# One image's store of a Winograd convolution, cut into transfers of 96, 24 and 8 channels

## The chip, the cores and the metric

The kernel runs on one core of one Trainium2 chip. The metric is the device time in microseconds, the median of several runs. One run was taken with the hardware profiler; its trace and profile page are what this document reads.

A core has five engines with instruction queues of their own: TensorE (PE, its weight loads PEld), VectorE (DVE), ScalarE (ACT), GpSimd (POOL) and SyncE (SP). Data moves by sixteen DMA engines, which all queues share. A transfer is issued from SP, ACT or POOL and cut into rows that are dealt out to the DMA engines; each DMA engine has a ring for each queue. In the profile, q1 is SP's queue, q10 ScalarE's, q0 GpSimd's; q8 and q14 bring instructions.

## The reference

A 3x3 convolution with padding 1, in fp32: sixteen images of 64 channels and 64x64 points, 128 channels out.

```python
batch, c_in, h, w, c_out = 16, 64, 64, 64, 128
x_pad = np.pad(x, ((0, 0), (0, 0), (1, 1), (1, 1)), mode='constant')
for kh in range(3):
    for kw in range(3):
        output[b, co] += weight[co, ci, kh, kw] * x_pad[b, ci, kh:kh+h, kw:kw+w]
```

The output is 16 x 128 x 64 x 64 in fp32, 33.55 MB; the input 16.8 MB.

## The kernel before

It is a Winograd form along the height, in fp16 with fp32 accumulation: two output rows are made from three sets of products instead of four. The images are taken in eight pairs (`p` from 0 to 7, `NP = 8`): the 64 channels of a pair's first image lie on partitions 0 to 63, those of the second on 64 to 127. Each pair has four blocks (`blk`) of eight row pairs.

Loading: `w_raw` and the first two pairs (`x0`, `x1`) come by SP's queue in fp32. Pairs 2 to 7 are loaded by GpSimd's queue, which casts them to fp16 (line 56); all six are issued in the first 8 us.

For each block, `group` makes three pairs of PSUM tiles on TensorE (line 159). ScalarE copies the first pair into `ut` (line 173), VectorE adds `ut` to the other two and writes the output tiles `ots` (lines 183 and 186). GpSimd forms the sums of row pairs `ss` that the first set reads.

Output tiles come from the pool `opool`, whose seven buffers are taken in turn: first by `x0` and `x1`, then by two tiles for each pair, eighteen times in all. One tile is a whole image: 128 channels (partitions) of 16 KB.

Storing: the first image of a pair is stored by SP's queue as soon as its last block is done (line 188). The second image's store is put into the list `held` and is issued from ScalarE's queue in the next block, right behind the two copies of line 173 (line 176). `cuts_of` says in which pieces: whole images for pairs 0 to 5 and for the second image of pair 6, halves of 32 output rows for the rest. `keep` keeps ScalarE's order as it is written. What is left in `held` is issued at the end (line 192).

The sixth pair is `p = 5`, so its second image is image 11 of 0 to 15. Its store is issued in pair 6, block 0.

Of the kernel before, what the change touches and what calls it, by code (L numbers as in the profile page):

```python
# [13 lines left out]
def kernel(  # L14
# [8 lines left out]
    CO = weight.shape[0]  # L23
    assert H == 64 and W == 64 and CI == 64 and CO == 128 and B % 2 == 0
    NP = B // 2
# [4 lines left out]
    out_rows = out.rearrange("b co h w -> b co h w")  # L30
# [34 lines left out]
    def sums(eng, p, src, lo, n):  # L65
        if p not in ss:
            ss[p] = spool.tile([128, H // 2, W], F16, tag="ss", name="ss")
        v = src.rearrange("p (j i) c -> p j i c", i=2)
        keep(
            eng.tensor_add(  # L70
                ss[p][:, lo : lo + n, :], v[:, lo : lo + n, 0, :], v[:, lo : lo + n, 1, :]
            )
        )
# [21 lines left out]
    def cast(copy, p, src, lo, hi):  # L95
        keep(copy(xs[p][:, lo:hi, :], src[:, lo:hi, :]))  # L96
# [13 lines left out]
    held = []  # L110
# [2 lines left out]
    halves = {1: (0, 32), 3: (32, 64)}  # L113
    cuts_of = [(whole, whole)] * (NP - 2) + [(halves, whole), (halves, halves)]

    def store(eng, p, b2, ot, lo, hi):
        return eng.dma_start(
            out_rows[2 * p + b2, :, lo:hi, :],
            ot.rearrange("p j i c -> p (j i) c")[:, lo:hi, :],
        )  # L120

    for p in range(NP):
        if p + 1 < NP:
            for lo in (0, 16):
                sums(nc.gpsimd, p + 1, x1 if p == 0 else xs[p + 1], lo, 16)
        ots = [
            opool.tile([128, H // 2, 2, W], F32, tag="ot", name="ot") for _ in range(2)
        ]
        for blk in range(4):
            j0 = blk * RB  # L130

            def group(wi_rows):

                tiles = [
                    psum.tile([128, RB, W], F32, tag="acc", name="acc") for _ in range(2)
                ]
                n = 3 * len(wi_rows)
                i = 0
                for wi, off in wi_rows:
                    for kw in (1, 0, 2):  # L140
                        c_lo, c_hi = max(0, 1 - kw), min(W, W + 1 - kw)
                        for b2 in range(2):
                            p0 = 64 * b2
                            lo, hi = j0, j0 + RB
                            if off is None:
                                rhs = ss[p][p0 : p0 + 64, lo:hi, c_lo + kw - 1 : c_hi + kw - 1]
                            else:
                                while 2 * lo + off < 0:
                                    lo += 1
                                while 2 * (hi - 1) + off > H - 1:  # L150
                                    hi -= 1
                                first = 2 * lo + off
                                last = 2 * (hi - 1) + off
                                rhs = xs[p][
                                    p0 : p0 + 64,
                                    first : last + 1 : 2,
                                    c_lo + kw - 1 : c_hi + kw - 1,
                                ]
                            nc.tensor.matmul(  # L159
                                tiles[b2][:, lo - j0 : hi - j0, c_lo:c_hi],  # L160
                                Wt[p0 : p0 + 64, wi, kw, :],
                                rhs,
                                start=i == 0,
                                stop=i == n - 1,
                            )
                        i += 1
                return tiles

            U = group([(G1, None)])
            us = []  # L170
            for b2 in range(2):
                ut = upool.tile([128, RB, W], F32, tag="ut", name="ut")
                keep(nc.scalar.copy(ut, U[b2]))  # L173
                us.append(ut)
            while held:
                keep(store(nc.scalar, *held.pop(0)))
            for piece in later.get((p, blk), ()):
                cast(nc.scalar.copy, *piece)
            if p == 0 and blk < 3:
                sums(nc.vector, 0, x0, j0 + RB, RB)  # L180
            A = group([(G21, 1), (G0, -1)])
            for b2 in range(2):
                nc.vector.tensor_add(ots[b2][:, j0 : j0 + RB, 0, :], A[b2], us[b2])  # L183
            Bt = group([(G01, 0), (G2, 2)])
            for b2 in range(2):
                nc.vector.tensor_add(ots[b2][:, j0 : j0 + RB, 1, :], Bt[b2], us[b2])  # L186
            if blk in cuts_of[p][0]:
                store(nc.sync, p, 0, ots[0], *cuts_of[p][0][blk])
            if blk in cuts_of[p][1]:
                held.append((p, 1, ots[1], *cuts_of[p][1][blk]))  # L190
    while held:
        keep(store(nc.scalar, *held.pop(0)))

# [29 lines left out]
```

## Time and profile before

| | |
|---|---|
| median of 3 runs | 126.64 us (126.49 to 126.67) |
| the profiled execution | 126.7 us, of which span 124.9 us |
| TensorE busy | 107.1 us (86%), granted clock 0.962 |
| VectorE busy | 83.4 us (67%) |
| ScalarE busy | 43.0 us (34%) |
| GpSimd busy | 36.9 us (30%) |
| HBM read and written | 17.07 MB and 33.55 MB |
| stores of 2048 KB from ACT's queue | 7, median 18.2 us from issue to landing |
| stores of 2048 KB from SP's queue | 6, median 19.2 us |
| stores of 1024 KB, SP and ACT | 4 and 2, median 9.2 and 8.3 us |

The span runs from the first to the last instruction of the program; what lies around it is the rest of the execution's time. Busy times are those of the compute engines; issuing a DMA does not count as busy. A DMA packet is one row as one DMA engine moves it, and each DMA engine that takes part in a transfer adds a packet of 4 bytes that signals its share as done.

### The profile page before, as it was taken

The numbers are of one execution on the slowest core, as the hardware profiler recorded it, in microseconds if no ns is written. First come the engines' busy times: TensorE is split into PE (matmuls) and PEld (weight loads), VectorE is DVE, ScalarE is ACT, GpSimd is POOL, SyncE is SP. The second block draws the span as 40 slices with busy tenths as digits, with TensorE's granted clock in tenths as the row PEclk, the third lists the DMA queues.
The fourth block names the chain that finished last, engine by engine and source line by source line (L and its number), as shares of the span: only waits on it lengthen the run. The fifth ranks groups of instructions, "written<-read, shape, count | busy, mean of one in ns | idle before, by whom it ended". The sixth has DMA issues, their size and how long they took to land.

```text
span 124.9 us, 2408 instructions
## 1 busy us (share of the span) xinstructions
PE 107.1 (86%) x978; PEld 53.9 (43%) x978; DVE 83.4 (67%) x134; ACT 43.0 (34%) x74; POOL 36.9 (30%) x29
## 2 busy tenths in 40 slices
PE   0489997399999999999999999999999999998000
PEld 0334443144545545555455555555555555553000
DVE  0135998227778777878877887877787778768200
ACT  4284234466333333333333333333333333333000
POOL 2845101999929101910048000750000000000000
PEclk9999999779999999999999999999999999999955
DMA  4999999999999999999999999999999999999991
GB/s 119 353 362 320 325 336 218 212 278 341 378 370 320 325 380 349 346 372 336 357 367 357 328 378 420 441 420 430 435 420 430 420 420 420 443 425 417 401 407 66
DMA packets 4187, 44.48 MB, mean 356 GB/s; under 512 B 465, under 2 KB 465, under 8 KB 721
## 3 DMA queue, kind: packets, MB, share of 16 engines
q1 hardware_dynamic: 2016, 21.27, 41.2%
q10 hardware_dynamic: 1296, 16.78, 31.7%
q0 software_dynamic: 864, 6.29, 24.3%
q8 instruction: 7, 0.11, 0.3%
q14 instruction: 4, 0.02, 0.0%
HBM read 17.07 MB, written 33.55 MB: 405 GB/s over the span
## 4 chain that ended last, share of the span: by engine, by line
PE 72%; DMA 15%; POOL 2%; DVE 1%; SPq 1%; issue 1%; DVEq 0%
PE acc L159 72%; DMA x<-in_x_dram 15%; POOL ss L70 2%; SPq L44 1%; DVE ot L183 1%; DVEq L218 0%; DVE ot L186 0%; SPq L41 0%; DVEq L183 0%
## 5 line engine op out<-in xcount | busy, mean ns | idle before, releaser
L159 PE MATMUL acc<-xs,Wt 64*128 64x504 f16 (+3 forms) x768 | 89.0, 379 | 0.0
L159 PEld LDWEIGHTS <-Wt 64*128 64x128 f16 x960 | 52.8, 96 | 56.2 <-issue 6.8
L183 DVE TENSOR_TENSOR ot<-acc,ut 128x512 f32<-128x512 f32 x64 | 41.2, 685 | 24.0 <-PE acc L159 21.7
L173 ACT COPY ut<-acc 128x512 f32<-128x512 f32 x64 | 34.4, 590 | 63.3 <-issue 41.7
L186 DVE TENSOR_TENSOR ot<-acc,ut 128x512 f32<-128x512 f32 x64 | 41.1, 683 | 0.0
L70 POOL TENSOR_TENSOR ss<-xs 128x1024 f16<-128x1024 f16 x12 | 25.2, 2125 | 31.7 <-DMA xs<-in_x_dram 31.7
L159 PE MATMUL acc<-ss,Wt 64*128 64x504 f16 (+1 forms) x192 | 27.6, 392 | 3.5 <-POOL ss L70 2.7
L70 DVE TENSOR_TENSOR ss<-x 128x512 f16<-128x512 f32 x4 | 2.7, 685 | 9.0 <-DMA x<-in_x_dram 9.0
L96 ACT CAST xs<-x 128x1024 f16<-128x1024 f32 (+1 forms) x6 | 6.3, 1067 | 3.1 <-DMA x<-in_x_dram 3.1
L70 POOL TENSOR_TENSOR ss<-x 128x1024 f16<-128x1024 f32 x2 | 4.7, 2344 | 8.4 <-DMA x<-in_x_dram 8.4
L88 PE MATMUL wp<-ident,w 128*64 128x128 f16 x18 | 1.3, 328 | 4.4 <-POOL w L50 4.4
L56 POOL DMA_DIRECT2D xs<-in_x_dram x6 | 3.3, 582 | 0.0
L96 POOL CAST xs<-x 128x1024 f16<-128x1024 f32 (+1 forms) x2 | 2.4, 1248 | 3.0 <-DMA x<-in_x_dram 3.0
L88 PEld LDWEIGHTS <-w 128*64 128x64 f16 x18 | 1.1, 210 | 4.4 <-POOL w L50 4.4
L90 ACT CAST Wt<-wp 128x384 f16<-128x384 f32 x1 | 0.5, 478 | 3.1 <-PE wp L88 3.1
L90 ACT ACT_TABLE_LOAD x1 | 1.3, 1283 | 0.7 <-PEq L207 0.7
L50 POOL CAST w<-w_raw 128x576 f16<-128x576 f32 x1 | 0.7, 663 | 2.4 <-DMA w_raw<-in_weight_dram 2.4
L99 ACT CAST Wt<-wp 128x384 f16<-128x384 f32 x1 | 0.5, 478 | 0.5 <-DVE Wt L93 0.5
L92 DVE TENSOR_TENSOR Wt<-wp,Wt 128x384 f16<-128x384 f32 x1 | 0.6, 550 | 0.0
L93 DVE TENSOR_TENSOR Wt<-wp,Wt 128x384 f16<-128x384 f32 x1 | 0.5, 547 | 0.0
L100 ACT CAST Wt<-wp 128x384 f16<-128x384 f32 x1 | 0.5, 485 | 0.0
masks.py:199 POOL TENSOR_SCALAR_AFFINE_SELECT ident<-ident 128x128 f16<-128x128 f16 x1 | 0.3, 292 | 0.1
(5 smaller groups left out, 0.6 us busy)
## 6 DMA issues: line engine op xcount, KB each, us to landing
out_dram<-ot ACTq DMA_DIRECT2D x7, 2048.0 KB, 18.2
out_dram<-ot SPq DMA_DIRECT2D x6, 2048.0 KB, 19.2
xs<-in_x_dram POOLq DMA_DIRECT2D x6, 1024.0 KB, 37.1
out_dram<-ot SPq DMA_DIRECT2D x4, 1024.0 KB, 9.2
x<-in_x_dram SPq DMA_DIRECT2D x1, 2048.0 KB, 19.3
out_dram<-ot ACTq DMA_DIRECT2D x2, 1024.0 KB, 8.3
x<-in_x_dram SPq DMA_DIRECT2D x1, 1472.0 KB, 9.0
x<-in_x_dram SPq DMA_DIRECT2D x1, 576.0 KB, 4.6
```

What stands on the lines that cost most here:

```text
L44: nc.sync.dma_start(x0[:, lo:hi, :], x_rows[0:128, lo:hi, :])
L50: keep(nc.gpsimd.tensor_copy(w16, w_raw))
L56: keep(nc.gpsimd.dma_start(xs[p], x_rows[128 * p : 128 * p + 128, :, :]))
L70: eng.tensor_add(ss[p][:, lo : lo + n, :], v[:, lo : lo + n, 0, :], v[:, lo : lo + n, 1, :])
L88: nc.tensor.matmul(wp[q : q + 64, k * CO : k * CO + CO], w16[:, t::9], ident)
L90: keep(nc.scalar.copy(wrow(G1), wps[1]))
L92: keep(nc.vector.tensor_sub(wrow(G21), wps[2], wrow(G1)))
L96: keep(copy(xs[p][:, lo:hi, :], src[:, lo:hi, :]))
L159: nc.tensor.matmul(tiles[b2][:, lo - j0 : hi - j0, c_lo:c_hi], Wt[p0 : p0 + 64, wi, kw, :], rhs, start=i == 0, stop=i == n - 1,)
L173: keep(nc.scalar.copy(ut, U[b2]))
L183: nc.vector.tensor_add(ots[b2][:, j0 : j0 + RB, 0, :], A[b2], us[b2])
L186: nc.vector.tensor_add(ots[b2][:, j0 : j0 + RB, 1, :], Bt[b2], us[b2])
```

## The change

The store of the sixth pair's second image is issued as three transfers instead of one: channels 0 to 95, 96 to 119 and 120 to 127, in this order, back to back on ScalarE's queue. 96 channels are dealt to sixteen DMA engines, six rows each; 24 to the first twelve, two each; 8 to the first eight, one each. So engines 0 to 7 move nine rows of this image, engines 8 to 11 eight and engines 12 to 15 six, where each moved eight. All other stores stay as they are.

```diff
-    def store(eng, p, b2, ot, lo, hi):
+    def store(eng, p, b2, ot, lo, hi, c0=0, c1=CO):
         return eng.dma_start(
-            out_rows[2 * p + b2, :, lo:hi, :],
-            ot.rearrange("p j i c -> p (j i) c")[:, lo:hi, :],
+            out_rows[2 * p + b2, c0:c1, lo:hi, :],
+            ot.rearrange("p j i c -> p (j i) c")[c0:c1, lo:hi, :],
         )
...
             if blk in cuts_of[p][1]:
-                held.append((p, 1, ots[1], *cuts_of[p][1][blk]))
+                edges = (0, 96, 120, CO) if p == NP - 3 else (0, CO)
+                for c in zip(edges, edges[1:]):
+                    held.append((p, 1, ots[1], *cuts_of[p][1][blk], *c))
```

## The prediction

> **What bounds the kernel now.** I read the chain of waits first, then the row of DMA shares on the page, then the queues, then windows over the last microseconds, then the single packets. The chain ends in the last addition, at 116.42 us, but the span is 124.9 us: 8.5 us follow in which no compute engine works, and SyncE's waits say for what (7.5 us for stores).
>
> ```profile
> span 124.9 us, 2408 instructions
> DMA  4999999999999999999999999999999999999991
> q1 hardware_dynamic: 2016, 21.27, 41.2%
> q10 hardware_dynamic: 1296, 16.78, 31.7%
> q0 software_dynamic: 864, 6.29, 24.3%
> q8 instruction: 7, 0.11, 0.3%
> SPq L218 <- DMA out_dram<-ot: 7.5, 4, 3.6
> ```
>
> The row of digits shows sixteen DMA engines busy from 2 us to 122 us. The queue shares add to 97.5% of sixteen engines over the span: 121.8 us of 124.9. So the end is set by when the last DMA engine has emptied its rings, and the other engines matter only if they fail to feed it. How evenly do the sixteen end? Windows answer (columns: stretch, length, busy of PE, PEld, DVE, ACT, POOL, clock, DMA share, GB/s).
>
> ```profile
> 115.70:116.10 0.40, 0.00 (x0) 0.00 (x0) 0.40 (x2) 0.00 (x0) 0.00 (x0) 1.00 0.97 410
> 116.10:116.40 0.30, 0.00 (x0) 0.00 (x0) 0.30 (x1) 0.00 (x0) 0.00 (x0) 1.00 0.78 328
> 116.40:116.70 0.30, 0.00 (x0) 0.00 (x0) 0.02 (x1) 0.00 (x0) 0.00 (x0) 1.00 0.78 328
> ...
> 121.30:121.60 0.30, 0.00 (x0) 0.00 (x0) 0.00 (x0) 0.00 (x0) 0.00 (x0) 0.50 1.03 437
> 121.60:121.90 0.30, 0.00 (x0) 0.00 (x0) 0.00 (x0) 0.00 (x0) 0.00 (x0) 0.50 0.59 246
> 121.90:122.20 0.30, 0.00 (x0) 0.00 (x0) 0.00 (x0) 0.00 (x0) 0.00 (x0) 0.50 0.58 246
> 122.20:122.50 0.30, 0.00 (x0) 0.00 (x0) 0.00 (x0) 0.00 (x0) 0.00 (x0) 0.50 0.39 164
> 122.50:122.80 0.30, 0.00 (x0) 0.00 (x0) 0.00 (x0) 0.00 (x0) 0.00 (x0) 0.50 0.20 82
> 122.80:123.10 0.30, 0.00 (x0) 0.00 (x0) 0.00 (x0) 0.00 (x0) 0.00 (x0) 0.50 0.13 55
> 123.10:123.40 0.30, 0.00 (x0) 0.00 (x0) 0.00 (x0) 0.00 (x0) 0.00 (x0) 0.50 0.07 27
> ```
>
> A window of 0.3 us counts the packets that begin in it, and with sixteen engines at work that is 437 GB/s, 27.3 for each. So 246 is nine engines, 164 six, 82 three, 55 two and 27 one. Seven engines are done by 121.8, the last nearly two microseconds later. In the windows at 116.1 to 116.7 some engines had even nothing to do: their rings were empty until the store issued at 115.85 arrived.
>
> The trace's packet records carry queue, start and length, but no engine number. On a busy engine the next packet starts 3 or 4 ns (in the loads up to 20 ns) before the last one ends, so from 5 us on the records string together into sixteen sequences. Their last records (4 bytes, the signal of completion) stand at 121.62 to 121.77 us (seven), 122.31, .44, .56, .59, .76, .77, .81 (seven), 123.27 and 123.49. Each of the seven instruction packets of queue 8 lies on another sequence: it takes 0.88 to 0.96 us, and the packet behind it, in five of seven cases, 0.98 to 1.02 instead of 0.61, so an engine loses about 1.3 us by it. Six of the seven middle engines have one; the seventh has two packets of queue 14, with 0.34 us of stall behind each. The engine that ends at 123.27, which I call T, has a queue 8 packet at 19.23 and 0.9 us of stalls in packets from 55.8 to 72.6 us. The last, S, has none, but from 75 to 113.5 us its 16 KB packets take 644 to 653 ns instead of 611. The seven early ones have neither.
>
> **The change, part by part.** Image 11's store (16 KB for each of 128 channels) goes out in pair 6, block 0, on ScalarE's queue, as three transfers instead of one.
>
> Issues. The row of before and its neighbours:
>
> ```profile
> 90.16 1.07 ACT L173 COPY ut<-acc 128x512 f32<-128x512 f32 x2 [2.09 <-issue]
> 90.84 0.34 ACTq L117 DMA_DIRECT2D out_dram<-ot  x1
> 93.34 1.07 ACT L173 COPY ut<-acc 128x512 f32<-128x512 f32 x2 [2.10 <-DVE ot L186]
> ```
>
> Two more issues of 0.34 us are 0.68 us, from 91.18 to 91.86. Behind them waits the copy of 93.34, which something else releases: 1.5 us of cover. Without it the copies, and so the additions that read them, would be 0.68 us late. The time taken is 0, at most 0.7 and nothing below zero, since nothing is issued earlier.
>
> Completion records. 12 and 8 more of 9 ns are at most 0.02 us on one engine.
>
> Buffers. Image 11's tile is the fourteenth taken from a pool of seven that is taken from eighteen times, so nobody reuses its buffer; when it lands matters only to the end. 0.
>
> Rows. This is the change. Engines 0 to 7 carry nine rows instead of eight, 8 to 11 eight, 12 to 15 six. A 16 KB row of a store takes 611 ns, started every 607. So engines 0 to 7 work 0.61 us longer, 12 to 15 1.21 less, and the bytes are the same. An engine that idled before 116.7 (0.26 to 0.54 us on six of the early ones) pays only the rest: if it is an early one, it ends at about 121.8 to 122.4 and does not matter. The time therefore hangs on one thing that the trace of before does not say outright: which numbers S and T have.
>
> Bounds. If S is one of 0 to 7, the end is 123.49 + 0.61 = 124.10: +0.61. If S is not but T is, 123.27 + 0.61 = 123.88: +0.39. If S is one of 8 to 11 and T not below 8, the end is S's as it was: 0. If S and T are both of 12 to 15 they end at 122.28 and 122.06, and a middle engine decides: untouched at up to 122.81, or, if it is one of 0 to 7, at 122.92 to 123.42. The best of all placings (seven early ones and the one of 122.31 in 0 to 7) ends at 122.92: -0.57. So the change lies between -0.57 and +0.61.
>
> Which way do numbers lean? Eight of sixteen places get the row, so with nothing known S is among them in half the cases, and else T in 8 of 15: 0.77 for slower. Against that speaks one stretch: the six idle engines began the store of 115.85 at 116.686, .697, .700, .713, .769 and .832, 0.84 to 0.98 us after its issue began, while the first weight load (issued at 0.74) began its first packet only at 1.741, after 1.00 us. If engines get a transfer in the order of their numbers, the early ones are numbers near 0, and 0 to 7 holds at most one or two late ones. A store and a cold load are not the same, so I give this order 0.6. Within it, nine late engines fill 7 to 15, and S or T at 7 costs; I put slower at 0.4 there and at 0.75 in every other order.
>
> [...]
>
> The sum for the likeliest case is +0.39 to +0.61; I take +0.5, since both ways in are about as likely. Against the profiled run, 124.9 us of span in 126.7, that is 127.2; that run lies 0.06 above the median of 126.64, so the median becomes 127.15.
>
> **The rivals.** (a) Faster: the two latest engines lie in 12 to 15, the middle ones mostly in 8 to 11, the early ones in 0 to 7. It decides when both S and T are at 12 or above; for it speaks the order of beginnings above, against it that no row ties S or T to a high number. End between 122.81 and 123.42, so -0.07 to -0.68, by the placings -0.57 at best: 126.1 to 126.55. (b) Nothing moves: S lies in 8 to 11, or a middle engine of 0 to 7 ends at 123.4 in place of S: 126.45 to 126.75. For it speaks only that five or six placings lead here. (c) The split is not the one it says: no transfer of before has fewer than 128 channels, so no row shows where 24 go. On eight engines, three each, engines 0 to 7 would carry ten rows, +1.22 us for S there: 127.9. [...]
>
> **How the numbers follow.** Slower: 0.6 x 0.4 + 0.4 x 0.75 = 0.54, with (c) in it. What is left goes about evenly between (a), 0.25, and (b), 0.21. A difference of 0.2% (0.25 us) is about what a measurement of this kernel can tell. The range reaches from 126.15, nearly the best placing, to 127.4, S's case with 0.15 for rates that shift with the load; outside stay (c) and the far ends, under 0.2. The slower case alone has 126.95 to 127.4.
>
> **What would show it.** In the changed profile queue 10 has 1316 packets instead of 1296; ScalarE's copy after the three issues starts no later against the matmuls before it. Right: the last windows thin out later, with one or two engines at 123.6 to 124, and the last sequence has nine rows of that store. Wrong: the last sequence has six or eight rows of it, or the sixteen end within a microsecond of each other; then the late engines had the high numbers. If a late engine shows slow packets in other places than S did, the lateness is not bound to a number and the placing argument falls.

## The result and the profile after

| | before | after |
|---|---|---|
| median | 126.66 us (126.49 to 127.26, 4 runs) | 131.38 us (131.23 to 131.58, 4 runs) |
| span of the profiled execution | 124.9 us | 129.5 us |

The ratio is 1.0365, with a 95% interval of 1.0328 to 1.0402: 4.7 us slower. Forecast were 127.15 us and a range up to 127.4.

The page of after, the same lines as of before:

```profile
span 129.5 us, 2410 instructions
DMA  4999999999999999999999999999999999999950
GB/s 127 328 374 289 336 326 215 218 291 369 364 364 321 339 395 359 347 331 390 347 362 352 334 385 450 425 415 445 425 400 354 319 296 392 428 422 420 428 218 35
q1 hardware_dynamic: 2016, 21.27, 40.5%
q10 hardware_dynamic: 1316, 16.78, 31.8%
q0 software_dynamic: 864, 6.29, 23.5%
```

Queue 10 has 1316 packets, as forecast: 36 signals where the one store had 16, which fits sixteen, twelve and eight engines. Which engines these are, and whether the eight are among the twelve, no record names; the rows for each engine and the numbers 0 to 15 were the author's assumption. The engines are as busy as before, but the row of rates has a dip (354, 319 and 296 in the 31st to 33rd of its 40 slices) where before it ran on at 420 to 430. Windows show the dip. Columns: stretch, length, busy of PE, PEld, DVE, ACT, POOL, clock, DMA share, GB/s. First before, then after:

```profile
88.00:96.00 8.00, 8.00 (x80) 4.15 (x76) 6.36 (x11) 2.22 (x5) 0.00 (x0) 1.00 1.01 428
96.00:104.00 8.00, 8.00 (x80) 4.11 (x77) 6.16 (x10) 3.18 (x6) 0.00 (x0) 1.00 0.99 421
104.00:112.00 8.00, 8.00 (x78) 4.05 (x76) 5.97 (x10) 2.19 (x5) 0.00 (x0) 1.00 1.01 428
```

```profile
88.00:96.00 8.00, 8.00 (x78) 4.31 (x76) 6.57 (x11) 2.86 (x6) 0.00 (x0) 1.00 1.01 422
96.00:104.00 8.00, 8.00 (x80) 4.29 (x78) 6.08 (x10) 2.51 (x5) 0.00 (x0) 1.00 1.02 339
104.00:112.00 8.00, 8.00 (x78) 4.23 (x76) 6.17 (x11) 2.80 (x6) 0.00 (x0) 1.00 1.00 380
```

A share of 1.02 with 339 GB/s says that the engines hold packets all the time and that the packets take longer. The packet records name them: from 80 us on, 54 store packets of 16 KB take more than 0.72 us, up to 2.53, all but one of them between 95 and 110 us; before one did (1.02 us, behind an instruction packet). From here on these are called long packets, and unless the text says otherwise they are counted from 80 us on. 40 of them are ScalarE's, the others belong to SyncE's stores, which were not changed and wait on the same DMA engines. The loss of rate over the two windows is (421 - 339)/421 x 8 + (428 - 380)/428 x 8 = 2.5 us for the sixteen engines together, and it is uneven:

```profile
122.00:123.00 1.00, 0.00 (x0) 0.00 (x0) 0.00 (x0) 0.00 (x0) 0.00 (x0) 0.50 1.01 426
123.00:124.00 1.00, 0.00 (x0) 0.00 (x0) 0.00 (x0) 0.00 (x0) 0.00 (x0) 0.50 0.82 344
124.00:125.00 1.00, 0.00 (x0) 0.00 (x0) 0.00 (x0) 0.00 (x0) 0.00 (x0) 0.50 0.55 229
125.00:126.00 1.00, 0.00 (x0) 0.00 (x0) 0.00 (x0) 0.00 (x0) 0.00 (x0) 0.50 0.29 123
126.00:127.00 1.00, 0.00 (x0) 0.00 (x0) 0.00 (x0) 0.00 (x0) 0.00 (x0) 0.50 0.23 98
127.00:128.00 1.00, 0.00 (x0) 0.00 (x0) 0.00 (x0) 0.00 (x0) 0.00 (x0) 0.50 0.12 49
```

Before, the last sequence of packets ended at 123.49 us; now it is 128.28, 4.8 us later, with a tail of five microseconds in which ever fewer engines work. Between 95 and 110 us the packets can be strung together in more than one way. By two of these ways the last sequence carries nine rows of image 11, and its long packets together run 4.4 or 5.7 us over their usual length.

The issues on ScalarE are no part of it. Its timeline:

```profile
88.88 1.07 ACT L173 COPY ut<-acc 128x512 f32<-128x512 f32 x2 [2.09 <-issue]
89.56 1.88 ACTq L117 DMA_DIRECT2D out_dram<-ot  x3
92.06 1.07 ACT L173 COPY ut<-acc 128x512 f32<-128x512 f32 x2 [2.10 <-DVE ot L186]
```

The three issues take 1.88 us together instead of three times 0.34, but the next copy starts after the same idle time of 2.10 us as before, released by the same addition.

Runs over 1.5% above the fastest of the same kernel are left out of the ratios, and of differences worked out from ratios, but not of the medians; the traces of e11_one_pair and e12_four_apart16 come from such runs (129.31 and 134.59 us), and in the last group of experiments (e9 to e12) the kernel before scattered from 126.53 to 128.17 us even without them, so that small differences of time say little there.

### The profile page after: what moved, and what is told of

Same layout as the page of the kernel before. It is cut to its first block, busy times and chain, and to the rows that moved or that the text cites. A ratio compares the mean times of both kernels' runs of the same rounds, so it can differ in the third digit from the quotient of the medians.

```text
span 129.5 us, 2410 instructions
## 1 busy us (share of the span) xinstructions
PE 105.8 (82%) x978; PEld 55.5 (43%) x978; DVE 83.4 (64%) x134; ACT 43.0 (33%) x74; POOL 37.0 (29%) x29
## 3 DMA queue, kind: packets, MB, share of 16 engines
q10 hardware_dynamic: 1316, 16.78, 31.8%
## 4 chain that ended last, share of the span: by engine, by line
PE 68%; DMA 15%; POOL 2%; DVE 1%; SPq 1%; issue 1%; DVEq 0%
PE acc L159 68%; DMA x<-in_x_dram 15%; POOL ss L70 2%; SPq L44 1%; DVE ot L183 1%; DVE ot L186 0%; DVEq L220 0%; SPq L41 0%; DVEq L183 0%
## 5 line engine op out<-in xcount | busy, mean ns | idle before, releaser
L159 PEld LDWEIGHTS <-Wt 64*128 64x128 f16 x960 | 54.4, 95 | 53.3 <-issue 4.9
L159 PE MATMUL acc<-ss,Wt 64*128 64x504 f16 (+1 forms) x192 | 27.1, 384 | 3.5 <-POOL ss L70 1.9
```

What stands on the lines that cost most here:

```text
L159: nc.tensor.matmul(tiles[b2][:, lo - j0 : hi - j0, c_lo:c_hi], Wt[p0 : p0 + 64, wi, kw, :], rhs, start=i == 0, stop=i == n - 1,)
```

## Experiments

Theory 1: in a transfer of 128 channels each DMA engine reads its own part of SBUF, the on-chip memory where the output tiles lie; cut by channels, several engines read the same part at once and stall each other and all that is queued behind. Theory 2: more transfers cost it, by issue or completion. Theory 3: the uneven rows cost it.

**Three transfers without a cut by channels** (e1_rows128).

```diff
-                held.append((p, 1, ots[1], *cuts_of[p][1][blk]))
+                lo, hi = cuts_of[p][1][blk]
+                edges = (0, 48, 60, 64) if p == NP - 3 else (lo, hi)
+                for r in zip(edges, edges[1:]):
+                    held.append((p, 1, ots[1], *r))
```

> Image 11 goes out in three transfers again, but each with all 128 channels, cut by output rows (0 to 47, 48 to 59, 60 to 63). Theory 1 (the cut by channels makes several DMA engines read the same part of SBUF, and they stall each other): no such sharing here, so 126.5 to 126.9, no packets of 16 KB pace above 0.7 us. Theory 2 (more transfers on ScalarE's queue cost the time, by their issue or completion): 131 as with the change. Theory 3 (only the uneven rows, nine, eight and six, cost): 126.5 to 126.9, as theory 1.

Measured 127.15 us against 126.83, ratio 1.0027 (1.0012 to 1.0043), and no long packet but one behind an instruction packet. Its windows show no dip:

```profile
96.00:104.00 8.00, 8.00 (x80) 4.23 (x77) 6.69 (x12) 2.38 (x5) 0.00 (x0) 1.00 0.99 413
104.00:112.00 8.00, 8.00 (x78) 4.17 (x76) 5.79 (x10) 2.99 (x6) 0.00 (x0) 1.00 1.02 430
```

Theory 2 falls as the cause of 4.7 us. The time is 0.25 us above the range of theories 1 and 3, though. Part of this small rest is packet length: a channel's 16 KB as packets of 12, 3 and 1 KB take 460 + 121 + 46 = 627 ns instead of 611, 0.13 us for eight rows.

**Even rows with a cut by channels** (e2_96_32): in the change, two transfers of 96 and 32 channels.

```diff
-                edges = (0, 96, 120, CO) if p == NP - 3 else (0, CO)
+                edges = (0, 96, CO) if p == NP - 3 else (0, CO)
```

> Image 11 in two transfers of 96 and 32 channels: six and two rows on each of sixteen engines, so eight on all, as before. Theory 1: the rows still lie on other engines than in a transfer of 128, so packets of 1 to 2.5 us come back and the time is 129 to 131.5. Theory 2: two thirds of the extra issues are there, at most half the loss, 128 to 129. Theory 3: no uneven rows, so 126.5 to 126.9 and no long packets.

Measured 130.12 us against 126.83, ratio 1.0258 (1.0219 to 1.0296), with 63 long packets. Its windows:

```profile
96.00:104.00 8.00, 8.00 (x80) 4.15 (x75) 6.55 (x11) 2.77 (x6) 0.00 (x0) 1.00 1.02 334
104.00:112.00 8.00, 8.00 (x78) 4.20 (x76) 5.59 (x10) 2.61 (x5) 0.00 (x0) 1.00 0.99 391
```

The same dip with eight rows on each engine, if 96 and 32 channels are dealt evenly to sixteen, which no record names: on that assumption theory 3 falls for 3.3 of the 4.7 us.

**The same rows, read four apart or as neighbours** (e3_four_own and e4_four_near). Both leave the stores as they were and add four transfers of eight channels behind image 11's store, to a spare tensor in HBM. Together they copy the same 32 partitions to the same 32 rows in both kernels, one row for each of eight engines in each transfer (queue 10 has 1360 packets in both, 64 more than before: eight rows and eight signals for each transfer); only which partitions go together differs.

```diff
+    spare = nc.dram_tensor("spare", (32, H, W), F32, kind="Internal").ap()
+    def extra(ot):
+        rows = ot.rearrange("p j i c -> p (j i) c")
+        for g in range(4):
+            keep(nc.scalar.dma_start(spare[8 * g : 8 * g + 8], rows[g : g + 29 : 4]))
...
                 job = held.pop(0)
                 keep(store(nc.scalar, *job))
+                if job[0] == NP - 3:
+                    extra(job[2])
```

The second kernel reads `rows[8 * g : 8 * g + 8]` instead.

> The kernel before, and behind image 11's store four more transfers of eight channels each, which copy 32 of its channels (partitions 0 to 31) to a spare place in HBM; each transfer takes every fourth partition. Four more rows of 16 KB on eight engines, 2.4 us. Theory 1: eight partitions four apart do not share, so the new packets take 0.61 to 0.65 us and the end moves by the rows alone: 128.3 to 129.3 where the slow engine S is among the eight, 127.9 to 128.7 where not. If short transfers stall whatever they read: over 130, with packets of 1 us and more.

> As the kernel with four own, with the same 32 partitions, the same spare rows of HBM and the same count of rows for each engine, but each transfer takes eight neighbouring partitions. Theory 1: four engines at a time read from one group of four partitions, a packet takes up to 4 x 0.61 = 2.4 us, so up to 7 us more on eight engines: 130 to 136, and at least 1 us above the kernel with four own. If HBM addresses or the number of engines in a transfer make the stalls: within 0.4 us of the kernel with four own.

Four own: 129.43 us against 126.83, ratio 1.0211 (1.0186 to 1.0237), no long packet but one behind an instruction packet; the time is a little above the expected 129.3. Four near: 132.46 us, ratio 1.0421 (1.0364 to 1.0477), with 19 long packets, up to 2.40 us, nearly four times 0.61. The two kernels' windows, four own first:

```profile
104.00:112.00 8.00, 8.00 (x76) 4.20 (x74) 6.18 (x11) 2.96 (x6) 0.00 (x0) 1.00 1.02 430
```

```profile
104.00:112.00 8.00, 8.00 (x76) 4.23 (x74) 6.18 (x11) 2.52 (x5) 0.00 (x0) 1.00 1.01 371
```

Bytes, HBM rows, transfers and rows for each engine are equal, so the 2.7 us between them (1.0421 against 1.0211) come from the SBUF side: theory 1 stands. Transfers on fewer than sixteen engines do not stall by themselves. Which partitions each engine reads in a transfer of 96, 64 or 24 channels stands in no record; that these stall for the same reason is inferred from packets of the same length (up to 2.53 us in after).

**The row term alone** (e5_one_own): one such transfer four apart.

> The kernel before and one extra transfer of eight channels four apart (partitions 0 to 28) to a spare place, behind image 11's store: one more row on each of eight engines, with no sharing. It is the row term of the prediction alone. If S (or T) is one of engines 0 to 7: +0.4 to +0.65 us, so 127.2 to 127.5. If neither is: within 0.25 us of the kernel before.

Measured 127.43 us against 126.80, ratio 1.0048 (1.0035 to 1.0061): +0.63 us. One row more on the eight engines is paid in full, so a latest engine is among them, and 0.61 was the right price of a row that is not disturbed. Four rows gave 2.60, 0.65 each.

**Two images** (e6_two_images): 96 and 32 channels for image 9 as well, `if p in (NP - 4, NP - 3)`.

> 96 and 32 channels for image 9 as well as image 11, eight rows on each engine for both. Theory 1 (sharing costs for as long as such rows are moved): twice the loss of one image, +5.5 to +7 us, 132.3 to 133.8, and about 120 long packets in place of 63. If the loss is a single disturbance that happens once (the queues fall out of step): +3.3 to +4 us, 130 to 130.8.

Measured 136.54 us against 126.80, ratio 1.0732 (1.0688 to 1.0777): +9.3 us by the ratio, nearly three times the loss of one image, with 178 long packets. It is no single disturbance, but twice was too little. Its windows:

```profile
88.00:96.00 8.00, 8.00 (x80) 4.04 (x78) 5.96 (x11) 2.74 (x6) 0.00 (x0) 1.00 1.00 287
96.00:104.00 8.00, 8.00 (x78) 4.07 (x76) 6.54 (x11) 2.66 (x6) 0.00 (x0) 1.00 1.01 313
```

The rate falls to 287, below what one image's worst window had (334). Why two cost more than double was not tried.

**Two at a time** (e7_four_pairs, e11_one_pair) **and one transfer of neighbours** (e10_one_near): the extra transfers with every second partition, four of them from partitions 0 to 31 (`rows[b : b + 15 : 2]` with b = 0, 1, 16, 17) or one (b = 0); and one of neighbours, `rows[0:8]`.

> The four extra transfers of eight channels from partitions 0 to 31 again, this time two apart (0, 2, ... 14 and so on), so that two engines at a time share a group of four partitions, where with neighbours there were four and with four own one. Theory 1 with a group as the unit: packets up to 2 x 0.61 = 1.22 us, none near 2.4, and a time between the two, 129.8 to 131.8. If it is not the group but only whether partitions are neighbours: as four own, 129.4, without long packets.

> One extra transfer of eight neighbouring channels (partitions 0 to 7) to a spare place: the row count of the kernel with one own, but four engines on each of two groups of four partitions. Theory 1: up to eight packets of 1.8 to 2.5 us (four rows at the pace of one) where one own has at most 1.01; +0.6 for the row and up to 1.8 for the stall, 128 to 129.5. If a stall needs several such transfers in a row: 127.4, as one own.

> One extra transfer of eight channels two apart (partitions 0 to 14): two engines on each group of four. Theory 1 with the count of engines as the price: packets of 1.0 to 1.5 us, none above 1.9, and 127.6 to 128.4. The packets above 2 us that the four transfers two apart had would then come from two transfers running into each other on the same four groups. If packets above 1.9 us appear here too, the count of engines on a group is not the price.

| kernel | extra rows | ScalarE packets of 16 KB over 0.72 us, from 100 us on | longest | ratio |
|---|---|---|---|---|
| e5_one_own | 8, four apart | 1 | 1.01 us | 1.0048 |
| e11_one_pair | 8, two apart | 4 | 1.07 us | 1.0029 (0.9989 to 1.0068) |
| e10_one_near | 8, neighbours | 6 | 2.27 us | 1.0037 (1.0000 to 1.0074) |
| e7_four_pairs | 32, two apart | 17 | 2.44 us | 1.0318 (1.0281 to 1.0355) |

Four pairs missed its bound of 1.22 us: the long packets that begin from 102.4 to 102.8 us, the first of the extra rows, take 1.03 to 1.51 us, and 2.0 to 2.4 come only from 103.9 to 104.5 us, when the next transfers run, the second on the same sixteen partitions as the first. That transfers run into each other there is an inference, since the records name neither the transfer nor the engine. One pair alone has no ScalarE packet near 2, which fits, though its packets are mostly shorter than expected and its time, 127.5 us by the ratio, lies just below its range. So a price by the count of engines on a group is not confirmed. One near has six long packets, but only two in the forecast 1.8 to 2.5 us, and the time is 127.57, not 128 to 129.5. A stall should reach the end only on an engine that ends late, while the slack of up to two microseconds takes it on an early one: strung together, the packet of 2.06 us lies on a sequence that ends at 122.96 us, 1.6 us before the last. That this is why the time missed is argued, not shown.

**Which partitions share** (e12_four_apart16 and e9_16_far): eight channels sixteen apart, `rows[g : g + 113 : 16]`, four times; sixteen channels four apart, `rows[g : g + 61 : 4]`, twice.

> Four extra transfers of eight channels that lie sixteen apart (0, 16, ... 112, then 1, 17 and so on): no two of a transfer in one group of four partitions. If the group of four is all that is shared: as four own, 129.2 to 129.7, no long packets. [...]

> Two extra transfers of sixteen channels four apart (partitions 0, 4, ... 60, then 1, 5, ... 61): two more rows on each of sixteen engines, +1.2 us. No two in one group of four. If the group is all that is shared: 127.9 to 128.4, no long packets. If partitions 32 apart share as well: engines in pairs, packets of 1.0 to 1.5 us, 128.6 to 130.

Four sixteen apart: ratio 1.0400 (1.0323 to 1.0476), 5.1 us on 127.13, with 29 long packets, the longest 2.64 us; counted as in the table it has 24. No two partitions of such a transfer are within a group of four, so groups of four are not all that is shared. The longest packet is over four times 0.61 us, and how many meet there no record says; all four transfers read the same eight groups of four partitions, as those of four own do with no long packet but one behind an instruction packet, and may overlap as in four pairs, which is not shown. Sixteen far: 128.71, ratio 1.0112 (1.0034 to 1.0191), eight ScalarE packets of 0.94 to 1.32 us, in the range for sharing in pairs, though the interval of the time does not exclude the other case.

**Two halves** (e8_64_64): image 11 in transfers of channels 0 to 63 and 64 to 127, `edges = (0, 64, CO)`.

> Image 11 in two transfers of 64 channels, partitions 0 to 63 and 64 to 127, four rows on each of sixteen engines, eight in all. Theory 1, if each half of the partitions is served by half of the paths: two engines on every path for all of the image, rows of up to 1.22 us, +2 to +5 us, 128.8 to 131.8. If only groups of four partitions count and each engine takes four neighbouring ones: no sharing, 126.6 to 127.1. Theory 3 (uneven rows): 126.6 to 127.1.

Measured 131.80 us against 126.80, ratio 1.0312 (1.0267 to 1.0356), 4.0 us by the ratio, with 86 long packets: eight rows on each engine, by the same assumption of an even deal, and even so a loss of the change's order.

Taken together: the packets of 16 KB of transfers of 128 channels took 0.61 us in the median of before; eight channels four apart from below partition 32 had no long packet but those behind an instruction packet; eight neighbours, eight sixteen apart and 64 neighbours had packets of up to 2.40, 2.64 and 2.28 us. Which partitions share with which beyond these cases is not shown.

## Why the prediction was wrong

Bound: right. The sixteen DMA engines set the end, and ScalarE's queue and the compute engines do not; the chain of compute work even ended 1.3 us earlier than before (115.14 against 116.42 us) and the end came later. Issues: right in effect, mis-sized (1.88 us for three, not 1.02), hidden as said. Completion records and buffers: nothing there that the runs contradict.

Rows: the step that failed, in one clause, "a 16 KB row of a store takes 611 ns", with "the bytes are the same". It took the row's price from transfers of 128 channels and kept it for a store cut by channels. There a row took 0.61 to 2.53 us, and the rows of SyncE's stores behind them waited too. So the bounds of -0.57 and +0.61 were no bounds: they held the counts of rows and not what is read at the same time. The numbering was bounded from both sides and the price was not, although rival (c) noted itself that no transfer of before has fewer than 128 channels.

The signs named for being right came true in part: queue 10's packets, the copy's idle time and the nine rows in the last sequence did, but instead of one or two engines at 123.6 to 124 us there were still 344 GB/s from 123 to 124. Nine rows in the last sequence fit the stalls as well, so that sign could not tell the two apart.

Numbering: it came out as forecast, but by luck. Slower had a chance of 0.54, hardly more than even, and the order of the first packets, which was given 0.6, spoke the other way. A latest engine was among the eight that get the extra row, and the row term came out at +0.63 where S gave +0.61. The forecast's sign came from this term; alone it would have given 127.3, so the term is about an eighth of what was measured, and most of the slowdown has a cause that the forecast did not have.

The sum as the runs have it: +3.3 us by cutting into 96 and 32 channels, +0.6 by the row, and 0.8 left of 4.7, for which the transfers of 24 and 8 neighbouring channels are the candidates (one of eight neighbours had packets up to 2.27 us); this part was not run by itself. The sum takes it that the parts simply add, which the two images, at nearly three times the loss of one, make doubtful. Rival (a) could not have won even with S and T on high numbers: the loss by sharing is larger than the best placing. Rival (c) is refuted by the packet count: three rows on each of eight engines would have given 1312, not 1316.

No run numbers the engines, so the order that was given 0.6 is neither shown nor refuted. What mattered was which partitions are read at the same time, and the prediction did not weigh it.

## What to carry to other kernels

Where DMA engines are the bound, as here, rows times the pace of a row gave a transfer's price (0.63 us for one row, 0.65 each for four) for transfers of 128 channels and for eight partitions four apart; for eight neighbours it did not, and a trace that shows only 128-partition transfers does not price a cut by partitions. Cut such a store by rows of the image instead, at 0.3% here against 2.6% for 96 and 32 channels. A share of 1.0 with a falling rate (here 1.02 at 339 GB/s against 0.99 at 421) is the sign to look for: the engines are busy, and the packets are long.

## What was not expected of the hardware

- Packets of unchanged stores on the other queue stall with the others (14 of 54 long packets in after, up to 1.99 us).
- Two images cost nearly three times what one costs (9.3 against 3.3 us).
- Three issues in a row on ScalarE's queue take 1.88 us together where one takes 0.34; in e1_rows128, with 128 channels each, the second and third take 2.24.
- In the kernels with pairs (e7 and e11), sixteen apart and sixteen far, three to five packets of SyncE's queue take 0.73 to 1.45 us near 92 us, ten microseconds before the extra rows move. Nothing that was run explains them.
